# Output projection by seven block products, its weight parts made in the first block, norm scaling on VectorE

## The chip, the cores and the metric

The kernel runs on one core of one Trainium2 chip. The metric is the device time of one execution in microseconds (us).

## What is computed

One hybrid encoder layer over 1024 tokens of 1024 channels, in float32. The reference, cut to what matters here:

```
h = LN1(alpha*x + 0.5*SwiGLU_a(x))
h = LN2(alpha*h + HybridMixer(h))
h = LN3(alpha*h + 0.5*SwiGLU_b(h))

def swiglu(x, w_gate, w_up, w_down):
    return (silu(x @ w_gate) * (x @ w_up)) @ w_down

# end of HybridMixer (after attention and the Fourier branch):
    merged = g_attn * (attn @ w_proj_attn) + g_four * (four @ w_proj_fourier)
    return merged @ w_out
```

`merged @ w_out`, the output projection, is the product that the change rewrites. The hidden width of each SwiGLU is 2752.

## The kernel before

**Precision.** TensorE takes float32 rounded (fp32r). Each operand is cut into a high part (a copy, on ACT, L346) and a low part (a subtraction, on VectorE, L350). A product is then three matmuls: high by high, low by high, high by low. A "split" below is that pair of operations on a page of 128x1024.

**Stages on TensorE (PE), in order.** The first SwiGLU block ("a"): 21 pair jobs for gate and up, then its down projection. Norm 1 and the transposes of its result (tpY). The values, queries, keys and gates (q, s, v pairs) with the attention. The projections of the two branches (pj, pf). The output projection (wo, L2078). Norm 2 and its transposes (tpZ, L407). The second block ("b"), norm 3 and the output.

**The down projection of block a** is done by seven products of blocks (Strassen-Winograd) and not by eight. Products come in the order 1, 6, 2, 5, 3, 7, 4, and each has eleven steps, j = 0 to 10. Each step has 12 matmuls (four token tiles m, three terms), and needs one page qa, loaded by SP in two transfers of 256 KB (L815 and L816, `load_step`) and then split. qa53 is step 3 of product 5. Results stay in PSUM bank sets: products 5 and 3 share set Z. Product 3 is added onto product 5's sum, so what VectorE has to take out of product 5 alone must be read in between. That is `a_p5` (L923, one per token tile), which adds bank Z onto the right half of `ya` of tile m+4:

```
        def a_p5(m):
            y = Y[m + 4][:, R]
            stt(y, y, ALPHA, B[tag, "Z", m], op0=OP.mult, op1=OP.add)
...
            jd(3, 0).after((p5, -2.5))
```

`ya` is the residual, the input row tile (512 KB), loaded by SP (L1089) in two groups: tiles 0 to 3, then tiles 4 to 7. The last line makes product 3's first step wait for `a_p5`. `a_c12` (L927) takes the finished Z, and norm 1 of tiles 0 to 3 follows it: a mean (L988), a Square with its sum and a square root on ACT (L993, L995), a reciprocal and a product on VectorE (L1004, L1005), the scaling on ACT (L1008), then transposes on PE and their evacuation on ACT (L417).

**What sets the order.** A planner writes out a static list of instructions for each engine from costs and due times; on the chip, each engine works through its list in order, and so does SP with the loads. SBUF is cut into 46 pages of 512 KB, and a load waits until its page is free. The wait can thus be for PE, VectorE or a store of POOL.

**Parts kept in DRAM.** `keep_parts` loads a weight page, splits it early, lets POOL store both parts (two transfers of 512 KB) and reloads both when they are needed (1 MB). Before the change it serves the eight pages of the branch weights w_proj_attn and w_proj_fourier, and its early work is due at step 8 of product 2 (`early = J["a", "d", 2, 8]`), with a lead of 60 us.

**The output projection** has 16 jobs (two halves of the channels, eight token tiles) of 24 matmuls. Its weights wo are loaded and split just ahead of it; each job's two banks are added to the residual on VectorE (L2085, L2087). The second block's first six weight pages ("ld") are loaded and split around its start by `lead_weights`.

Of the kernel before, what the change touches and what calls it, by code (L numbers as in the profile page):

```python
# [16 lines left out]
P = 128  # L17
# [278 lines left out]
def kernel(  # L296
# [3 lines left out]
    w_proj_attn, w_proj_fourier, w_out, ln2_g, ln2_b, ffn2_gu, ffn2_tail,  # L300
# [8 lines left out]
    b_in, w_pa, w_pf, w_out = b_in[0], w_proj_attn[0], w_proj_fourier[0], w_out[0]  # L309
# [30 lines left out]
    def split(name, get, put, deps=(), need=None, lead=14.0, w=1024, pages=2, gives=1):  # L340

        st = {}

        def hi():
            st["h"] = page(name + "h", F32R)
            nc.scalar.activation(st["h"][:, :w], get()[:, :w], AF.Copy)  # L346
# [6 lines left out]
        if isinstance(need, tuple):  # L353

            def piece(i):
                cs, last = slice(i * 512, (i + 1) * 512), None

                def hi_():
                    if i == 0:
                        st["h"] = page(name + "h", F32R)  # L360
                    nc.scalar.activation(st["h"][:, cs], get()[:, cs], AF.Copy)

                def lo_():
                    if i == 0:
                        st["l"] = page(name + "l", F32R)
                        put((st["h"], st["l"]))
                    nc.vector.tensor_sub(st["l"][:, cs], get()[:, cs], st["h"][:, cs].bitcast(F32))
# [16 lines left out]
    class Operand:  # L384
# [12 lines left out]
        def turn(self, m, node, tile_of, c0):  # L397
# [11 lines left out]
            for q in range(2):  # L409
                n = f"a{hf + 1}{q + 1}"  # L410
                for i in range(2):
                    def evac(n=n, i=i, q=q):
                        if (n, i) not in self.raw:
                            self.raw[n, i] = page(f"{self.name}{n}{i}")
                        for j in range(2 * i, 2 * i + 2):
                            k = c0 + 4 * q + j
                            nc.scalar.activation(self.raw[n, i][:, (j % 2) * 512 + col * P:(j % 2) * 512 + (col + 1) * P],  # L417
                                                 ps[q][:, j, :], AF.Identity, bias=ln_cols[:, k + 8:k + 9],
                                                 scale=ln_cols[:, k:k + 1])
                    self.got.setdefault((n, i), []).append(S(0.56, evac, [f], frees=i, pages=1 if col == 0 else 0))  # L420

        def derive(self, first, whole, lead):
# [3 lines left out]
            def parts(n, i, deps, need, src=None, gives=0):  # L426
                self.node[n, i] = split(f"{self.name}{n}{i}", lambda: raw[src or n, i],
                                        lambda p: self.part.__setitem__((n, i), p), deps, need,
                                        lead if need is first.get(n) else 14.0, gives=gives)
                return self.node[n, i]  # L430
            for n in ("a11", "a12", "a21", "a22"):
                for i in range(2 if first[n] else 0):
                    if isinstance(got[n, i], tuple):
                        self.node[n, i] = parts(n, i, got[n, i], (first[n], first[n]))
                    else:
                        parts(n, i, got[n, i], first[n])
# [185 lines left out]
    def ffn(tag, X, w_gu, w_tail, w_dn, load_rest, norm, rest_deps=None, sums_at=None, by_tile=False):  # L622
# [5 lines left out]
        LEAD = 6  # L628
# [123 lines left out]
        for i, c in enumerate(ck[:LEAD]):  # L752
            lead_weights(c, w_gu, J[c0, 1], ((41.0 if i == 0 else 38.6 - 0.2 * i), 37.0 - 0.2 * i) if tag == "a" else None)
# [227 lines left out]
    def norm_head(acc, sums, deps, name, which):  # L981
# [14 lines left out]
        n = V(0.12, mean, deps)  # L996
        return st, n, S(1.7, dev, [n], pages=1)

    def norm_tile(acc, sums, deps, name, which):

        st, _, n = norm_head(acc, sums, deps, name, which)
# [5 lines left out]
        def scaled():  # L1007
            nc.scalar.activation(st["y"], st["a"], AF.Identity, bias=sums()[:, 2:3], scale=st["rs"])  # L1008
        n = V(0.3, shift, [n])
        return S(1.4, scaled, [n], gives=1), lambda: st["y"]  # L1010
# [50 lines left out]
    X1, X2, X3 = Operand("X"), Operand("Y"), Operand("Z")  # L1061
# [604 lines left out]
    branch_jobs((0, 1, 2, 3, 4), (0,))  # L1666
    branch_jobs((5,), (1, 2))
    branch_jobs((6,), (3,))
    branch_jobs((7,), (4, 5))
    for gi in range(2):  # L1670
        for m in range(8):
            WJ[gi, m] = job(24 * MM, None, 2, gives=16 if m == 7 else 0)
            if gi == 0 and m < 2:
                branch_jobs((), (6 + m,))
# [6 lines left out]
    def keep_parts(name, load, deps, fold_=None):  # L1681
# [22 lines left out]
        def again(key, need, lead):  # L1704
            def run():
                PW[key] = t = page(name + "h", F32R), page(name + "l", F32R)
                for i in range(2):
                    nc.sync.dma_start(t[i].bitcast(F32), dst[i])
            q = Q(need, 1.0, run, [(n, 6.0)], lead, pages=2)
            need.after(q)  # L1710
        return again
    PW, kept = {}, {}
    for c2 in range(4):
# [17 lines left out]
        kept["f", c2] = keep_parts(f"wpf{c2}", load_pf, [(rev_n, 20.0)], fold_w)  # L1731

# [245 lines left out]
    pj_n = {}  # L1978
# [23 lines left out]
    for c in range(8):  # L2002
# [27 lines left out]
        def sine(c=c, st=st):  # L2030
            st["q"] = half(f"pfq{c}")
            nc.scalar.activation(st["q"], st["s"], AF.Copy)

# [12 lines left out]
        def merge(c=c, st=st):  # L2046
            nc.vector.tensor_add(gates[0, c], gates[0, c], st.pop("f"))
        q = gate_load(1, c, FJ[c])
        n = S(0.62, sine, [FJ[c]], frees=1, halves=1)
        n = V(1.8, outs, [n], frees=2, hgives=1, pages=1)  # L2050
        n = V(1.23, gate, [n, q], gives=1)
        n = V(1.23, merge, [n] + pj_n[c], gives=1)
        split(f"mg{c}", lambda c=c: gates[0, c], lambda p, c=c: merged.__setitem__(c, p), [n],
              WJ[c // 4, 0], 100.0)


    wo = {}
    for k in range(8):
        def load(k=k):
            wo[k] = t = page(f"wo{k}")  # L2060
            nc.sync.dma_start(t, w_out[k * P:(k + 1) * P, :])
        split(f"wo{k}", lambda k=k: wo[k], lambda p, k=k: wo.__setitem__(k, p),
              [Q(WJ[k // 4, 0], 0.5, load, (), pages=1)], WJ[k // 4, 0])
    for m in range(8):
        st, sums = {}, kb.small([P, 4], "lw", bufs=9)

        def load(m=m, st=st):
            st["a"] = t = page(f"ya{m}")
            nc.sync.dma_start(t, y_spill[m])
        q = Q(WJ[0, m], 0.5, load, [(spilled[1, m], 5.0)], pages=1)  # L2070
        for gi in range(2):
            def run(gi=gi, m=m, st=st):
                st["b", gi] = bk = [bank(f"wo{gi}{m}{i}") for i in range(2)]
                ms = slice(m * P, (m + 1) * P)
                for k in range(4 * gi, 4 * gi + 4):
                    for ti, (a, b) in enumerate(TERMS):
                        for i in range(2):
                            nc.tensor.matmul(bk[i], pick(merged[k], a)[:, ms], pick(wo[k], b)[:, i * 512:(i + 1) * 512],  # L2078
                                             start=(k == 4 * gi and ti == 0), stop=(k == 4 * gi + 3 and ti == 2))
            WJ[gi, m].fn = run  # L2080

        def add(gi, i, m=m, st=st, sums=sums):
            a = st["a"][:, i * 512:(i + 1) * 512]
            if gi == 0:
                stt(a, a, ALPHA, st["b", 0][i], op0=OP.mult, op1=OP.add)  # L2085
            else:
                stt(a, st["b", 1][i], 1.0, a, op0=OP.mult, op1=OP.add, accum_out=sums[:, i:i + 1])  # L2087
        deps = []
        for i in range(2):
            n = V(0.69, lambda i=i, add=add: add(0, i), [WJ[0, m], q], frees=1)  # L2090
            deps.append(V(0.69, lambda i=i, add=add: add(1, i), [WJ[1, m], n], frees=1))
        n, y = norm_tile(lambda st=st: st["a"], lambda sums=sums: sums, deps, f"y2_{m}", 2)
        unit[2, m] = G(lambda m=m, y=y: pool_dma(n2_spill[m], y()), [n])
        X3.turn(m, n, y, 16)
# [7 lines left out]
    def rows2(ck):  # L2102
# [6 lines left out]
        rows2, lambda k: (J[PC["q", k], 1], J[PC["q", k], 4]), True)  # L2109
# [46 lines left out]
def _layouts(inputs):  # L2156
# [6 lines left out]
    for i in (1, 2):  # L2163
# [17 lines left out]
    out["c_ln"] = np.concatenate([a[f"ln{i}_{w}"].reshape(KD, P).T for i in (1, 2) for w in "gb"], 1)  # L2181
    out["in_values"] = v.transpose(3, 0, 2, 1, 4).reshape(3, 4, P, 1024)
# [4 lines left out]
        "w_proj_attn", "w_proj_fourier", "w_out", "ln2_g", "ln2_b", "ffn2_gu", "ffn2_tail",  # L2187
# [21 lines left out]
```

## Time and profile before

| what | value |
|---|---|
| time, median of 3 runs | 2071.83 us (2071.36 to 2073.81) |
| the profiled execution | 2072.24 us, span 2070.3 us |
| TensorE busy | 2058.5 us of the span, granted clock 0.999 |
| VectorE, ACT, POOL busy | 1276.4, 910.4, 233.6 us |
| down projection of block a, product 5 | 509.85 to 539.77 us |
| output projection, first to last matmul | 1339.7 to 1439.6 us |
| traffic | 401.29 MB, mean 194 GB/s |

A row of the stretches in the prediction gives a stretch, its length, each engine's busy time with the number of its instructions, the granted TensorE clock, the share of time that the 16 DMA engines are busy (a little over 1 where packets overlap) and GB/s. A row of the waits gives the instruction that waits, what it waits for, the sum, how often, and the longest. A timeline row begins with the start and the duration.

### The profile page before, as it was taken

Reading aid. Unit: us, or ns where it says so; the run is one execution under the profiler, and the core shown is the slowest. Engines: PE = TensorE matmul, PEld = TensorE weight load, DVE = VectorE, ACT = ScalarE, POOL = GpSimd, SP = SyncE. Lnnn points to the kernel's source line nnn. Section 1 sums busy time; section 2 is a strip of 40 time slices with the busy share of each in tenths; the row PEclk is TensorE's granted clock in tenths of the full one; section 3 lists DMA queues with packets and bytes.
Section 4 is the critical chain, followed back from the end, with each engine's and each line's share of the span. In section 5 each row is a group of like instructions: output and inputs, shape, how many; then the busy total and the mean of one; then the engine's idle time right before and its main releaser. Section 6 shows DMA issues by size and latency. Waiting matters only on the chain.

```text
span 2070.3 us, 25541 instructions
## 1 busy us (share of the span) xinstructions
PE 2058.5 (99%) x9523; PEld 1713.6 (83%) x9523; DVE 1276.4 (62%) x1757; ACT 910.4 (44%) x1441; POOL 233.6 (11%) x404
## 2 busy tenths in 40 slices
PE   9999999999999999999999999999999999999998
PEld 7888888888888888888888888888888888888887
DVE  7865555576554658455556764763877665575565
ACT  6433333555475324455455443318633333355342
POOL 0122111010000010021121111000011101010000
PEclk9999999999999999999999999999999999999999
DMA  5778875599743336467786659523144433357743
GB/s 203 236 239 260 253 220 169 177 341 404 257 160 120 102 122 182 142 178 204 207 218 198 226 185 384 184 97 138 60 169 179 157 132 127 123 202 273 263 159 105
DMA packets 151292, 401.29 MB, mean 194 GB/s; under 512 B 18338, under 2 KB 40690, under 8 KB 150720
## 3 DMA queue, kind: packets, MB, share of 16 engines
q1 hardware_dynamic: 111648, 266.38, 37.2%
q0 software_dynamic: 39520, 133.28, 21.5%
q8 instruction: 74, 1.21, 0.2%
q14 instruction: 50, 0.41, 0.1%
HBM read 303.41 MB, written 153.84 MB: 221 GB/s over the span
## 4 chain that ended last, share of the span: by engine, by line
PE 97%; ACT 1%; DMA 1%; DVE 0%; issue 0%; DVEq 0%; SPq 0%
PE Ab L462 14%; PE Aa L462 13%; PE Aq L462 8%; PE Da L462 6%; PE Db L462 5%; PE As L462 5%; PE wo L2078 3%; PE Dq L462 3%; PE Zb L827 3%; PE Xb L827 3%; PE Za L827 3%; PE Xa L827 3%; PE pj L1991 2%; PE v L1238 2%; PE Ds L462 2%; PE pv L1600 2%
## 5 line engine op out<-in xcount | busy, mean ns | idle before, releaser
L1568 ACT ACTIVATE p<-p,stat 128x192 f32<-128x192 f32 (+2 forms) x96 | 42.3, 442 | 17.0 <-DVE stat L1563 16.0
L326 POOL DMA_DIRECT2D hsaa<-t2a x21 | 12.0, 571 | 317.1 <-DVE t2a L696 299.0
L1358 DVE SCALAR_TENSOR_TENSOR oq<-Dq,b_cols,t2q 128x512 f32<-128x512 f32 x12 | 11.8, 986 | 50.8 <-PE Dq L462 50.8
L326 POOL DMA_DIRECT2D hsba<-t2b x21 | 11.4, 543 | 279.6 <-DVE t2b L696 279.6
L1600 PEld LDWEIGHTS pv<-pT,v 128*128 128x128 f32 (+1 forms) x320 | 37.3, 189 | 6.1 <-ACT pT L1589 1.0
L692 DVE TENSOR_TENSOR t2b<-Db,t2b 128x512 f32<-128x512 f32 x21 | 14.5, 691 | 44.9 <-PE Db L462 44.9
L692 DVE TENSOR_TENSOR t2a<-Da,t2a 128x512 f32<-128x512 f32 x21 | 14.5, 691 | 44.4 <-PE Da L462 44.4
L600 ACT ACTIVATE t2a<-Aa 128x512 f32<-128x512 f32 x21 | 12.6, 600 | 65.5 <-PE Aa L462 65.4
L1600 PE MATMUL pv<-pT,v 128*128 128x128 f32 (+1 forms) x320 | 40.8, 289 | 0.5 <-ACT pT L1589 0.5
L600 ACT ACTIVATE t2b<-Ab 128x512 f32<-128x512 f32 x21 | 12.6, 599 | 62.9 <-PE Ab L462 62.9
L1553 DVE SCALAR_TENSOR_TENSOR p<-sc,bias 128x512 f32<-128x512 f32 (+1 forms) x40 | 24.7, 620 | 25.0 <-PE sc L1539 20.6
L326 POOL DMA_DIRECT2D n_spill<-y x16 | 8.6, 538 | 264.5 <-ACT y L1008 264.5
L1539 PE MATMUL sc<-oq,oq 128*128 128x192 f32 (+2 forms) x192 | 34.1, 322 | 0.0
L684 DVE TENSOR_TENSOR t3a<-Da,t3a 128x512 f32<-128x512 f32 x21 | 14.5, 690 | 27.8 <-PE Da L462 26.4
L1539 PEld LDWEIGHTS sc<-oq,oq 128*128 128x128 f32 x192 | 29.8, 190 | 2.0
L1358 DVE SCALAR_TENSOR_TENSOR oq<-Dq,b_cols,t3q 128x512 f32<-128x512 f32 x12 | 11.8, 987 | 30.1 <-PE Dq L462 30.1
L462 PE MATMUL Db<-Zs40h,usb 128*128 128x512 f32 x84 | 29.4, 391 | 0.7 <-DVE t3b L684 0.7
L462 PE MATMUL Db<-Zs41h,usb 128*128 128x512 f32 x84 | 29.3, 389 | 0.0
L462 PE MATMUL Da<-Xs40h,usa 128*128 128x512 f32 x84 | 29.3, 389 | 0.0
L462 PE MATMUL Da<-Xs41h,usa 128*128 128x512 f32 x84 | 29.3, 389 | 0.0
L684 DVE TENSOR_TENSOR t3b<-Db,t3b 128x512 f32<-128x512 f32 x21 | 14.5, 690 | 20.7 <-PE Db L462 16.0
L1563 DVE TENSOR_REDUCE stat<-p 128x2 f32<-128x384 f32 (+2 forms) x40 | 24.5, 620 | 1.2
(7340 smaller groups left out, 7210.4 us busy)
## 6 DMA issues: line engine op xcount, KB each, us to landing
qa<-hsas SPq DMA_DIRECT2D x44, 256.0 KB, 5.9
qa<-tdat SPq DMA_DIRECT2D x44, 256.0 KB, 5.4
qb<-hsbs SPq DMA_DIRECT2D x44, 256.0 KB, 4.4
ga<-in_ffn_gu_dram SPq DMA_DIRECT2D x21, 512.0 KB, 6.1
ua<-in_ffn_gu_dram SPq DMA_DIRECT2D x21, 512.0 KB, 8.4
gb<-in_ffn_gu_dram SPq DMA_DIRECT2D x21, 512.0 KB, 3.5
ub<-in_ffn_gu_dram SPq DMA_DIRECT2D x21, 512.0 KB, 4.4
qa<-hsaa SPq DMA_DIRECT2D x33, 256.0 KB, 4.8
```

The lines of the kernel that those rows point to most:

```text
L326: nc.gpsimd.dma_start(*a, **kw)
L462: nc.tensor.matmul(out, pick(w, a)[:, k * P:(k + 1) * P], self.cols(xn, b, k), start=first and k == 0 and ti == 0, stop=last and k == 3 an ...
L600: nc.scalar.activation(H[c, t], B[c, "B"], AF.Copy)
L684: nc.vector.tensor_sub(H[c, "t3"], B[c, "D"], H[c, "t3"])
L692: nc.vector.tensor_sub(H[c, "t2"], B.pop((c, "D")), H[c, "t2"])
L827: nc.tensor.matmul(B[tag, set_, m], pick(q, a)[:, m * P:(m + 1) * P], pick(q, b)[:, R], start=first and j == 0 and ti == 0, stop=j == PAIR ...
L1238: nc.tensor.matmul(ps, X2.cols(f"a{hf + 1}{k // 4 + 1}", a, k % 4)[:, mm * P:(mm + 1) * P], pick(wv, b), start=(k == 0 and ti == 0), stop= ...
L1539: nc.tensor.matmul(sv[:, i, :], qk[0][:, qt * P:(qt + 1) * P], qk[1][:, k0:k0 + w], start=True, stop=True, skip_group_check=True)
L1568: nc.scalar.activation(p3()[:, i, :], p3()[:, i, :], AF.Exp, bias=stats[h][:, k, 0:1], scale=1.0, accum_out=stats[h][:, k, 1:2])
L1600: nc.tensor.matmul(out_of(tiles.index(qt)), env["v"][kc, rows], pt[r0:r0 + rows, sl * P:(sl + 1) * P], start=qt not in seen, stop=last, sk ...
L1991: nc.tensor.matmul(bk[hf], pick(wv, a)[:, k, cc * P:(cc + 1) * P], pick(attn[k], b)[:, hf * 512:(hf + 1) * 512], start=(k == 0 and ti == 0 ...
L2078: nc.tensor.matmul(bk[i], pick(merged[k], a)[:, ms], pick(wo[k], b)[:, i * 512:(i + 1) * 512], start=(k == 4 * gi and ti == 0), stop=(k == ...
```

## The change

1. **Seven products.** The output projection uses the same seven block products, in the order 1, 2, 6, 7, 5, 4, 3, each with four jobs of 12 matmuls. The merged operand becomes raw pages ("M"), with splits and 1024-wide combinations of blocks on VectorE (`X4.derive`). The sums of w_out's blocks are made on the chip, by a copy and an adding DMA each, during block a's pair jobs 13 to 17. Four copies on ACT seed the second bank of products 6 and 7 with product 1's result, and 24 additions on VectorE take the place of 32.

```
    WORDER = ((1, "A", True), (2, "A", False), (6, "B", False), (7, "B", False), (5, "D", True), (4, "B", False),
              (3, "D", False))
    for p, bk, new in WORDER:
        for m in range(4):
            WJ[p, m] = job(12 * MM, None, int(new), gives=8 if m == 3 else 0)
```

2. **Parts made in block a.** Fourteen parts of w_out (wob: blocks, wot: sums of blocks) and the second block's six pages (wl) go through `keep_parts`. The loads of wo and ld, and their splits, are gone from the place of use; reloads of 1 MB each stand there.

```
    lead2 = [keep_parts(f"wl{c}", lambda t, c=c: nc.sync.dma_start(t, ffn2_gu[c, 0]), [],
                        early=J["a", "d", 7, 8]) for c in range(LEAD)]
    for r, (p, _, _) in enumerate(WORDER):
        n = PROD[p][1]
        for i in range(2):
            kept["o", n, i] = keep_parts(f"wo{n}{i}", lambda t, n=n, i=i: nc.sync.dma_start(t, out_block(n)[i]),
                                         [wtn[n]] if n in wtn else [], early=J["a", "d", (5, 3, 7)[r // 3], 8])
```

3. **Norm 1 and norm 2.** The scaling moves from ACT to VectorE, and so does half of the evacuation of the transposes; the planner gets a slack for them, and norm 2 serves tiles 0 to 3 first.

```
-            nc.scalar.activation(st["y"], st["a"], AF.Identity, bias=sums()[:, 2:3], scale=st["rs"])
+            nc.vector.tensor_scalar(st["y"], st["a"], st["rs"], sums()[:, 2:3], op0=OP.mult, op1=OP.add)
...
+                            if q == 0:
+                                nc.scalar.activation(dst, ps[q][:, j, :], AF.Identity, bias=b_, scale=g_)
+                            else:
+                                nc.vector.tensor_scalar(dst, ps[q][:, j, :], g_, b_, op0=OP.mult, op1=OP.add)
```

Three places show how the order moves. In the lists, `[waits DMAHW..]` is a load's landing, `DMASW` a store's.

SP's loads just ahead of the second group of ya, before (qa_4191 is step 2 of product 3, qa_4208 and qa_4229 are steps 3 and 4):

```order
L815 DMA qa_4191<-hsas_174 128x512 [waits DMAHW1_49,DVE_49]
L816 DMA qa_4191<-in_ffn_down_dram 128x512 [waits DMAHW2_49]
L815 DMA qa_4208<-hsas_175 128x512 [waits DMAHW3_49,PE_49]
L816 DMA qa_4208<-in_ffn_down_dram 128x512 [waits DMAHW4_49]
L815 DMA qa_4229<-hsas_176 128x512 [waits DMAHW5_49,PE_49]
L816 DMA qa_4229<-in_ffn_down_dram 128x512 [waits DMAHW6_49]
L1089 DMA ya_4252<-in_x_dram 128x1024 [waits DMAHW7_49,PE_49]
```

and of the change (qa_4318 and qa_4335 are steps 3 and 4):

```order
L1768 DMA wot_4290<-wtt_259 128x1024 [waits DMAHW5_49,DVE_49]
L1768 DMA wot_4292<-wtt_259 128x1024 [waits DMAHW6_49,PE_49]
L1768 DMA wot_4294<-wtt_257 128x1024 [waits DMAHW7_49,DMASW2_49]
L1768 DMA wot_4296<-wtt_257 128x1024 [waits DMAHW0_49,DMASW4_49]
L1768 DMA wot_4298<-wtt_260 128x1024 [waits DMAHW1_49,DVE_49]
L1768 DMA wot_4300<-wtt_260 128x1024 [waits DMAHW2_49,DMASW5_49,DMASW0_49]
L827 DMA qa_4318<-hsas_175 128x512 [waits DMAHW3_49,DMASW7_49,DMASW6_49]
L828 DMA qa_4318<-in_ffn_down_dram 128x512 [waits DMAHW4_49]
L827 DMA qa_4335<-hsas_176 128x512 [waits DMAHW5_49,DMASW7_49]
L828 DMA qa_4335<-in_ffn_down_dram 128x512 [waits DMAHW6_49]
L1101 DMA ya_4356<-in_x_dram 128x1024 [waits DMAHW7_49,PE_49]
```

Six loads of parts have come between steps 2 and 3, some with waits for POOL's stores; a first group of six (wob and wot) stands further ahead, after step 2 of product 5.

VectorE at a_p5, before (L923):

```order
L350 TENSOR_TENSOR qa310l<-qa_4359,qa310h 128x1024 [waits DMAHW5_49,DMAHW6_49,DVE_49,Activation_49]
L350 TENSOR_TENSOR qa70l<-qa_4380,qa70h 128x1024 [waits DMAHW0_49,DMAHW7_49,DVE_49,Activation_49]
L923 SCALAR_TENSOR_TENSOR ya_4252<-ya_4252,Za_4263 128x512 [waits PE_49]
L923 SCALAR_TENSOR_TENSOR ya_4254<-ya_4254,Za_4264 128x512 [waits PE_49]
L923 SCALAR_TENSOR_TENSOR ya_4256<-ya_4256,Za_4265 128x512 [waits PE_49]
L923 SCALAR_TENSOR_TENSOR ya_4258<-ya_4258,Za_4266 128x512 [waits PE_49]
L350 TENSOR_TENSOR qa71l<-qa_4401,qa71h 128x1024 [waits DMAHW1_49,DMAHW2_49,DVE_49,Activation_49]
```

and of the change (L935):

```order
L350 TENSOR_TENSOR wot41el<-wot_4300,wot41eh 128x1024 [waits DMAHW2_49,Activation_49]
L350 TENSOR_TENSOR qa33l<-qa_4318,qa33h 128x1024 [waits DMAHW3_49,DMASW6_49,DMAHW4_49,DVE_49,Activation_49]
L350 TENSOR_TENSOR qa34l<-qa_4335,qa34h 128x1024 [waits DMAHW5_49,DMAHW6_49,DVE_49,Activation_49]
L935 SCALAR_TENSOR_TENSOR ya_4356<-ya_4356,Za_4367 128x512 [waits DMAHW7_49,PE_49]
L935 SCALAR_TENSOR_TENSOR ya_4358<-ya_4358,Za_4368 128x512 [waits DMAHW0_49,PE_49]
```

Before, the splits stood eleven and more steps ahead (product 7's first step) when a_p5 came, and a_p5 waited for PE alone; now the last split ahead of it is step 4 of product 3, and a_p5 waits for the landing of ya too.

VectorE at a_c12, of the change (L939; before, the split ahead of it was that of qa40):

```order
L350 TENSOR_TENSOR qa72l<-qa_4546,qa72h 128x1024 [waits DMAHW3_49,DMASW5_49,DMAHW4_49,DVE_49,Activation_49]
L350 TENSOR_TENSOR wl0el<-wl_4549,wl0eh 128x1024 [waits DMAHW5_49,PE_49,Activation_49]
L350 TENSOR_TENSOR wl1el<-wl_4551,wl1eh 128x1024 [waits DMAHW6_49,DVE_49,Activation_49]
L350 TENSOR_TENSOR wl2el<-wl_4569,wl2eh 128x1024 [waits DMASW7_49,DMAHW7_49,PE_49,Activation_49]
L350 TENSOR_TENSOR wl3el<-wl_4571,wl3eh 128x1024 [waits DMAHW0_49,DVE_49,Activation_49]
L350 TENSOR_TENSOR wl4el<-wl_4573,wl4eh 128x1024 [waits DMASW1_49,DMAHW1_49,PE_49,Activation_49]
L350 TENSOR_TENSOR wl5el<-wl_4575,wl5eh 128x1024 [waits DMAHW2_49,DVE_49,Activation_49]
L939 SCALAR_TENSOR_TENSOR ya_4214,lsa<-Za_4367,ya_4214 128x512 [waits PE_49]
```

The six splits of wl have come ahead of a_c12. On PE, the transposes of tiles 0 and 1 (tpY) now stand before step 3 of product 7; before, they stood after it.

More of the change, by code (lines that the diff above doesn't have):

```diff
@@ L308 @@
     x, out = x[0], out[0]
-    b_in, w_pa, w_pf, w_out = b_in[0], w_proj_attn[0], w_proj_fourier[0], w_out[0]
+    b_in, w_pa, w_pf, w_out = b_in[0], w_proj_attn[0], w_proj_fourier[0], out_blocks
     def as_k(t, kd=KD):
@@ L338, in pick, with split @@
         return parts[0 if kind == "hi" else 1]
-    def split(name, get, put, deps=(), need=None, lead=14.0, w=1024, pages=2, gives=1):
+    def split(name, get, put, deps=(), need=None, lead=14.0, w=1024, pages=2, gives=1, tokens=False):
         st = {}
@@ L353, in split, with cut @@
         if isinstance(need, tuple):
+            def cut(t, i):
+                return t.rearrange("p (k n) -> p k n", k=2)[:, :, i * 256:(i + 1) * 256] if tokens else t[:, i * 512:(i + 1) * 512]
             def piece(i):
[L356 removed]
                 def hi_():
@@ L979, in root_table, with norm_head @@
         S(1.5, lambda: nc.scalar.activation(t, eps, AF.Sqrt), [after_])
-    def norm_head(acc, sums, deps, name, which):
+    def norm_head(acc, sums, deps, name, which, slack=4.0):
         st = {}
@@ L995, in dev, with norm_tile @@
             nc.scalar.activation(st["rs"], s[:, 3:4], AF.Sqrt, bias=eps, scale=1.0 / D)
[L996 to L1001, printed above, removed]
+        n = V(0.12, mean, deps, slack=slack)
+        return st, n, S(1.75, dev, [n], pages=1, slack=slack)
+    def norm_tile(acc, sums, deps, name, which, slack=4.0):
+        st, _, n = norm_head(acc, sums, deps, name, which, slack)
         def shift():
@@ L1702, in keep_parts, with again @@
         fl.later(n, 6.0, gives=2)
-        def again(key, need, lead):
+        def again(key, need, lead, got=None):
             def run():
@@ L1712, with out_block, copy, add @@
     PW, kept = {}, {}
+    oblk = {f"b{kh + 1}{nh + 1}": w_out[2 * kh + nh] for kh in range(2) for nh in range(2)}
+    wt = {n: kb.dram([2, P, 1024], f"wt{n}") for n in ("t1", "t2", "t3", "t4")}
+    wtn = {}
+    def out_block(n):
+        return (oblk if n in oblk else wt)[n]
+    for i, (to, x0, x1) in enumerate((("t1", "b11", "b12"), ("t3", "b12", "b22"), ("t2", "t1", "b22"),
+                                      ("t4", "t2", "b21"))):
+        def copy(to=to, x0=x0):
+            nc.sync.dma_start(wt[to], out_block(x0))
+        def add(to=to, x1=x1):
+            pool_dma(wt[to], oblk[x1], accum_op=OP.add, max_dma_last_dim=4096)
+        n = Q(J[("a", 13 + i), 1], 1.0, copy, [wtn[x0]] if x0 in wtn else [], lead=0.0)
+        wtn[to] = Q(J[("a", 14 + i), 5], 1.0, add, [n], lead=0.0)
     for c2 in range(4):
@@ L2057 @@
[L2057 to L2063, printed above, removed]
-    for m in range(8):
[L2065 to L2092, printed above, removed]
@@ new lines, with run @@
+        n = V(1.38, merge, [n] + pj_n[c], gives=2, pages=2 if cc == 0 else 0)
+        for r in (1, 2):
+            X4.got.setdefault((f"a{r}{c // 4 + 1}", c % 4 // 2), []).append(n)
+    X4.derive({"a11": WJ[1, 0], "a12": WJ[2, 0], "a21": None, "a22": WJ[4, 0]}, {p: WJ[p, 0] for p in PROD}, 30.0)
+    for p, bk, new in WORDER:
+        xn, wn = PROD[p]
+        for i in range(2):
+            kept["o", wn, i](("o", wn, i), WJ[p, 0], 22.0 - 2.0 * i)
+        WJ[p, 0].after(X4.nodes(xn))
+        for m in range(4):
+            def run(p=p, bk=bk, new=new, m=m, xn=xn, wn=wn):
+                if new:
+                    B["w", bk, m] = bank(f"w{bk}{m}")
+                for k in range(4):
+                    w = [t[:, (k % 2) * 512:(k % 2) * 512 + 512] for t in PW["o", wn, k // 2]]
+                    for ti, (a, b) in enumerate(TERMS):
+                        nc.tensor.matmul(B["w", bk, m], X4.cols(xn, a, k)[:, m * P:(m + 1) * P], pick(w, b),
+                                         start=new and k == 0 and ti == 0, stop=k == 3 and ti == 2,
+                                         skip_group_check=True)
+            WJ[p, m].fn = run
```

130 lines of the change are left out of this document (96 added, 34 removed).

## The prediction

> **What bounds the kernel now.** I read the page first: busy shares, the traffic by slices, then the chain that ended last.
>
> ```profile
> span 2070.3 us, 25541 instructions
> PE 2058.5 (99%) x9523; PEld 1713.6 (83%) x9523; DVE 1276.4 (62%) x1757; ACT 910.4 (44%) x1441; POOL 233.6 (11%) x404
> GB/s 203 236 239 260 253 220 169 177 341 404 257 160 120 102 122 182 142 178 204 207 218 198 226 185 384 184 97 138 60 169 179 157 132 127 123 202 273 263 159 105
> PE 97%; ACT 1%; DMA 1%; DVE 0%; issue 0%; DVEq 0%; SPq 0%
> ```
>
> PE is busy for all but 11.8 us and is 97% of the chain. A matmul removed is time removed, unless something else then makes PE wait. The traffic row says where that could be: slices 9 and 10 (414 to 518 us) carry 341 and 404 GB/s, far over the mean. Next, PE's waits:
>
> ```profile
> PE Db L462 <- DVE t3b L684: 0.7, 1, 0.7
> PE tpZ L407 <- ACT y L1008: 0.6, 3, 0.2
> ```
>
> So the kernel holds no wait worth removing, and no slack that absorbs a new one. Last, the traffic around those two slices, which lie in the first block's down projection, where the change puts its new transfers (columns: stretch, length, busy time of each engine, PE clock, DMA share, GB/s):
>
> ```profile
> 430.00:460.00 30.00, 30.00 (x135) 24.82 (x134) 17.46 (x17) 14.76 (x14) 1.65 (x4) 1.00 1.08 328
> 460.00:490.00 30.00, 30.00 (x134) 24.86 (x133) 17.46 (x17) 13.26 (x15) 6.83 (x13) 1.00 1.04 413
> 490.00:520.00 30.00, 30.00 (x134) 24.85 (x133) 24.39 (x29) 17.20 (x17) 0.00 (x0) 1.00 1.04 396
> 520.00:540.00 20.00, 20.00 (x90) 16.53 (x89) 10.56 (x11) 11.46 (x11) 0.00 (x0) 1.00 0.98 342
> 540.00:580.00 40.00, 40.00 (x178) 33.14 (x177) 22.70 (x38) 18.70 (x24) 0.53 (x1) 1.00 0.58 183
> 580.00:640.00 60.00, 60.00 (x283) 50.17 (x282) 30.39 (x51) 34.85 (x63) 3.52 (x7) 1.00 0.34 123
> ```
>
> The DMA engines are full (share 0.98 to 1.08) until 540, and PE still never waits: SP is running ahead of it. That lead is the only cushion.
>
> **The matmuls removed.** One down product of 132 matmuls lasts from 509.85 to 539.77:
>
> ```profile
> 509.85 0.39 PE L827 MATMUL Za<-qa50h 128*128 128x512 f32 x1
> 539.77 0.39 PE L827 MATMUL Za<-qa30h 128*128 128x512 f32 x1
> ```
>
> 29.92/132 = 0.2267 us each; a step of 12 is 2.72. The output projection goes from 8×2×24 = 384 to 7×4×12 = 336 matmuls: 48×0.2267 = **−10.88 us**. The 0.6 us of tpZ's wait on ACT goes with the scaling that leaves ACT: **−0.6** (bounds −0.6 and +1, if VectorE is late instead).
>
> **Work added to VectorE in the projection.** Its rows:
>
> ```profile
> 1305.00:1340.00 35.00, 35.00 (x195) 30.58 (x195) 28.40 (x44) 12.48 (x16) 0.00 (x0) 1.00 0.44 160
> 1340.00:1440.00 100.00, 99.36 (x474) 82.62 (x473) 53.07 (x107) 47.78 (x91) 3.26 (x6) 1.00 0.31 114
> L2047 DVE TENSOR_TENSOR gl<-gl,prf 128x1024 f32<-128x1024 f32 x8 | 9.8, 1225 | 0.3
> L2087 DVE SCALAR_TENSOR_TENSOR ya<-wo,ya 128x512 f32<-128x512 f32 x16 | 10.5, 689 | 14.1 <-PE wo L2078 14.1
> L1880 DVE SCALAR_TENSOR_TENSOR fcl<-fp,f_se,fch x4: 352/352/353, 1290.3 to 1299.8; 128x128 fp32r<-128x128 f32 x4
> L1942 DVE CAST fmidT<-fmidT x1: 420/420/420, 1304.9 to 1304.9; 4x514 fp32r<-4x514 f32 x1
> ```
>
> VectorE has 81.5 us there now. Added: 8 wide combinations at 1.225 (9.8), 32 transposed evacuations of 128x128 out of PSUM at 0.352 (11.3), 8 scalings. No row shows a 1024-wide scaling from SBUF with one tensor input: twice the 514-wide cast gives 0.84, the two-input row 1.23, and I take 0.84, the nearer in kind (6.7). Gone: 8 of the 32 adds (5.5) and two of 16 splits (2.4). That makes 101 us in 124, 82%: a busy engine, not yet the bound. Walking PE's and VectorE's new orders side by side with these durations (an estimate), the tightest places are the second tile's normed rows, 0.7 us ahead of their transposes, and the copies into the third product's banks, 1.2 ahead. I cost this at 0, bounds 0 and +3 (0.4 us more on each of eight scalings).
>
> **The transfers added.** Twenty parts (14 of w_out, 6 of the second block) are each loaded (0.524 MB), split, stored (two of 0.524 MB) in the first block, and reloaded later (1.05 MB). The reloads add 21 MB in about 150 us around the projection, 140 GB/s on the 160 and 114 above: below 396, hidden. The sums of w_out's blocks add some 8.4 MB over 80 us in slices 4 and 5 (260 and 253 GB/s): about 360, hidden, bounds 0 and +2. The loads and stores in the full stretch are not hidden. Order there: 6 parts, seven steps, four ya, four steps, 6 parts, two steps, and only then the four ya that a_p5 (now L935) needs. a_p5 must read bank Z before product 3 writes to it. Before:
>
> ```profile
> L1089 SPq DMA_DIRECT2D ya<-in_x_dram x8: 328/328/333, 498.2 to 513.4; - x8
> DMA to landing us min/median/max: 5.9/6.9/7.8
> 537.93 2.73 DVE L923 SCALAR_TENSOR_TENSOR ya<-ya,Za 128x512 f32<-128x512 f32 x4 [3.80 <-PE Za L827]
> ```
>
> The last ya is issued at 513.4 and lands 6.9 later, at 520.3; the fourth a_p5 starts at 540.0 (537.93 plus three of 0.68). Margin: 19.7 us. Ahead of that landing the change puts 12 loads (6.29 MB) and the first group's 12 stores (6.29 MB). The engines carried 396 GB/s there without room left, so 12.58/0.396 = **31.8 us** later: 552.1, **12.1 us past the need**. The second group's stores can push in as well, up to 15.9 us more. That stores don't wait politely is in the trace, from 460 to 490, when the parts of w_pa and w_pf were stored:
>
> ```profile
> DMA packets 4709, 12.38 MB, mean 413 GB/s; under 512 B 529, under 2 KB 532, under 8 KB 4708
> q0 software_dynamic: 2096, 7.60, 62.2%
> q1 hardware_dynamic: 2612, 4.76, 41.2%
> 470.16 1.06 ACT L346 ACTIVATE qa25h<-qa 128x1024 fp32r<-128x1024 f32 x1 [2.57 <-DMA qa<-in_ffn_down_dram]
> 473.94 1.06 ACT L346 ACTIVATE qa26h<-qa 128x1024 fp32r<-128x1024 f32 x1 [0.77 <-DMA qa<-in_ffn_down_dram]
> ```
>
> POOL's stores (q0; columns: packets, MB, share) took 61% of the bytes; a step of SP's came every 3.8 us where PE uses one in 2.72. SP is also held back by pages: in the new order its loads of the second group wait for POOL's stores of the first. I take half of the second group's stores ahead, since their last splits come when the ya are already queued: **+20.0 us** (bounds 12.1 and 28.0).
>
> The Trainium skill, page "DMA: Bandwidth & Descriptors", section "Queues, rings and completion order", says that each DMA engine takes turns between queues with work, a packet at a time. The trace agrees: 2096 and 2612 packets, though the bytes stand 61 to 38. The same page, section "Specifications", limits a core's HBM traffic to about 358 GB/s; by that 12.58 MB would take 35.1 us and not 31.8, and the stall would be 3.3 longer. The row of 413 GB/s over 30 us speaks against it here, so the sum goes by 396.
>
> **The next thing late.** After a_p5 the new VectorE order puts six splits of the second block's weights (wl0 to wl5) ahead of a_c12, from which norm 1 and the transposes before product 7's fourth step follow:
>
> ```profile
> 567.85 0.69 DVE L927 SCALAR_TENSOR_TENSOR ya<-Za,ya 128x512 f32<-128x512 f32 x1 [7.56 <-PE Za L827]
> 573.64 0.16 DVE L1004 RECIPROCAL lnrs<-lnrs 128x1 f32<-128x1 f32 x1 [0.29 <-ACT lnrs L995]
> ```
>
> From 560 SP has 9 steps (4.7 MB) and six wl (3.1) to bring beside 3.1 to 6.2 of stores: 27.7 to 35.6 us, so the last wl is split at 590 to 598. a_c12 falls due at 567.9+20 = 587.9. Its rows are wanted 10.0 us after that (577.85: product 7 begins 29.92 after 539.77, and three steps follow) and take 7.4 (573.64, two small operations, a scaling): 2.5 us of cover. I take **+4 us**, bounds 0 and +8.
>
> **Sum**, against the profiled execution's own 2072.24 (the span and 1.94 around it, which stay; 0.41 over the median of 2071.83): 2072.24 −10.88 −0.6 +20.0 +4 = 2084.8, so **2085**. Bounds: 2072.24−11.5+12.1 = 2072.9 and 2072.24−11.5+28+8 = 2096.8.
>
> **The rivals.**
> *The stores give way* (faster). If SP's loads alone go first, the last ya lands at 520.3+15.9 = 536.2, inside the need of 540.0, and the whole −11.5 stands: 2060.8. It decides at 3.8×0.396 = 1.5 MB of stores ahead of that landing. For it: stores do queue, and took up to 15.2 us to land. Against it: the 61% above.
>
> ```profile
> wpa_d<-wpa1el POOLq DMA_DIRECT2D x1, 512.0 KB, 6.7
> wpf_d<-wpf3el POOLq DMA_DIRECT2D x1, 512.0 KB, 15.2
> ```
>
> Chance 0.15.
> *The stall about cancels the gain.* If half of the first group's stores go ahead (23.8 us), the last ya lands at 544.1, 4.1 late; with 4 to 8 at the norm: 2069 to 2073. Chance 0.15.
> *The third group hurts as well.* Its 16 stores (8.4 MB) at 7.60/30 = 253 GB/s last 33 us, in which product 7's steps come every 3.8 us and not 2.72: 8.8 steps × 1.06 = 9 us more, 2094. It decides once SP's lead is under three steps when product 7 begins. Chance 0.17.
> *Seven products don't shorten the projection* because VectorE becomes its bound: +3 on a case without the DMA stall, 2064. Against it: 82%. Chance 0.03.
> The forecast has 0.50.
>
> **How the numbers follow.** 2085 is the likeliest case. The range 2064 to 2098 leaves out the first rival (0.15) and about 0.05 above. A measurement here tells about 0.2% (4.1 us) from no change: faster means below 2067.7, the first and the last rival, 0.18; same is 2067.7 to 2076, the second, 0.15; slower 0.67.
>
> **What would show it.** Right: in the waits, a_p5 on VectorE waits some 20 us for the DMA of ya near 540, PE's Za waits on that a_p5, the DMA share stays at 1 to about 600 instead of 540, and a second, smaller PE wait stands at tpY or at product 7's steps; the projection is 10.9 us shorter and without waits. Wrong: ya landed before 540 with PE at 100% in the down projection (first rival), or PE waits at tpZ or at the third product's banks.

## The result, and the profile after

The changed kernel takes **2089.60 us** (median of 6 runs, 2087.29 to 2094.34) against 2071.86 us (6 runs, 2071.36 to 2073.81): a ratio of **1.0088, 95% interval 1.0075 to 1.0101**. It is slower, inside the range, 4.6 us over the forecast of 2085. The profiled execution took 2093.08 us, its span is 2091.0.

The page after, with the lines that answer to those of before:

```profile
span 2091.0 us, 25730 instructions
PE 2055.6 (98%) x9475; PEld 1707.6 (82%) x9475; DVE 1329.1 (64%) x1855; ACT 885.5 (42%) x1375; POOL 258.8 (12%) x448
GB/s 201 244 239 258 256 260 256 175 336 412 409 400 262 96 147 114 184 147 190 210 203 223 206 213 308 267 262 247 86 173 159 176 142 110 125 201 279 262 169 93
PE 87%; DMA 11%; DVE 1%; ACT 1%; issue 0%; SPq 0%; POOL 0%; DVEq 0%; ACTq 0%; POOLq 0%
```

PE's share of the chain has fallen from 97% to 87%, and DMA's has risen from 1% to 11%. Two slices far over the mean have become four (9 to 12, 418 to 627 us, 336 to 412 GB/s), and slices 6 and 7 rose from 220 and 169 to 260 and 256. PE's own waits:

```profile
PE Za L839 <- DVE ya L935: 19.6, 4, 17.0
PE Aa L470 <- ACT t3a L608: 3.6, 1, 3.6
PE Ua L839 <- DVE qa40l L350: 0.8, 1, 0.8
PE Ua L839 <- DVE qa41l L350: 0.7, 1, 0.7
PE tpY L409 <- DVE y L1020: 0.6, 2, 0.4
```

The first is a_p5, the bank that product 3 has to wait for. The second is new and was not forecast. No wait at tpZ is left. The stretches of the down projection:

```profile
490.00:520.00 30.00, 30.00 (x134) 24.86 (x133) 19.70 (x19) 14.87 (x14) 6.35 (x12) 1.00 1.04 410
520.00:540.00 20.00, 20.00 (x90) 16.57 (x89) 8.63 (x14) 5.99 (x6) 0.00 (x0) 1.00 1.04 409
540.00:580.00 40.00, 20.43 (x71) 14.86 (x71) 22.38 (x24) 15.62 (x16) 6.38 (x12) 0.70 1.03 403
580.00:640.00 60.00, 58.35 (x270) 47.41 (x269) 42.14 (x65) 37.80 (x54) 12.54 (x23) 1.00 1.03 402
```

The DMA share stands at 1.03 until 640 (before, 0.58 and 0.34 in the last two rows), and PE works 20.4 of the 40 us from 540 to 580, at a mean clock of 0.70. What a_p5 waited for, on its line and on the line that loads ya:

```profile
L935 DVE SCALAR_TENSOR_TENSOR ya<-ya,Za x4: 686/689/689, 561.6 to 569.2; 128x512 f32<-128x512 f32 x4
  DMA ya<-in_x_dram: 5.6, 4
...
L1101 SPq DMA_DIRECT2D ya<-in_x_dram x8: 327/328/333, 519.7 to 551.5; - x8
...
DMA to landing us min/median/max: 11.0/14.0/17.6
```

The last ya is issued at 551.5 (before: 513.4) and takes up to 17.6 us (before: 7.8). The fourth a_p5 starts at 569.2 instead of 540.0. VectorE's own wait for ya is only 5.6 us, because it stands at the splits of qa33 and qa34 first. Their loads come just ahead of ya in SP's queue and land late too:

```profile
560.24 1.23 DVE L350 TENSOR_TENSOR qa34l<-qa,qa34h 128x1024 fp32r<-128x1024 f32 x1 [2.56 <-ACT qa34h L346]
561.63 0.69 DVE L935 SCALAR_TENSOR_TENSOR ya<-ya,Za 128x512 f32<-128x512 f32 x1 [0.17 <-DMA ya<-in_x_dram]
```

Where the time went, by the first matmul of each stage in both traces:

| first matmul | before | after | later by |
|---|---|---|---|
| down projection of block a (qa10) | 420.1 | 425.6 | 5.5 |
| product 5 (qa50) | 509.9 | 515.3 | 5.4 |
| product 3 (qa30) | 539.8 | 562.5 | 22.7 |
| product 7 (qa70) | 569.7 | 599.5 | 29.8 |
| values | 633.1 | 665.7 | 32.6 |
| queries | 791.7 | 825.4 | 33.7 |
| branch projections (pj) | 1262.3 | 1296.0 | 33.7 |
| second block | 1439.6 | 1459.3 | 19.7 |
| its down projection | 1853.3 | 1873.8 | 20.5 |
| end of the span | 2070.3 | 2091.0 | 20.7 |

So: 5.5 in the pair jobs, 24.4 around a_p5, 3.9 from product 7 to the queries, −14.0 from the projections to the second block, and 0.8 lost again in the second block before its down projection.

### The profile page after: what moved, and what is told of

It reads as the page before. It is cut to its first block, busy times and chain, and to the rows that moved or that the text cites. A ratio compares the mean times of both kernels' runs of the same rounds, so it can differ in the third digit from the quotient of the medians.

```text
span 2091.0 us, 25730 instructions
## 1 busy us (share of the span) xinstructions
PE 2055.6 (98%) x9475; PEld 1707.6 (82%) x9475; DVE 1329.1 (64%) x1855; ACT 885.5 (42%) x1375; POOL 258.8 (12%) x448
## 4 chain that ended last, share of the span: by engine, by line
PE 87%; DMA 11%; DVE 1%; ACT 1%; issue 0%; SPq 0%; POOL 0%; DVEq 0%; ACTq 0%; POOLq 0%
PE Ab L470 14%; PE Aa L470 13%; PE Aq L470 8%; PE Db L470 5%; PE Da L470 5%; PE As L470 5%; DMA qa<-tdat 4%; PE Dq L470 3%; DMA qa<-in_ffn_down_dram 3%; PE Zb L839 3%; PE Xb L839 3%; PE pj L2029 2%; PE Ds L470 2%; PE v L1250 2%; PE wA L2118 2%; PE pv L1612 2%
## 5 line engine op out<-in xcount | busy, mean ns | idle before, releaser
L326 POOL DMA_DIRECT2D hsaa<-t2a x21 | 12.1, 574 | 313.4 <-DVE t2a L705 313.4
L1551 PEld LDWEIGHTS sc<-oq,oq 128*128 128x128 f32 x192 | 29.8, 190 | 2.0
```

Source lines behind the costliest of these rows:

```text
L326: nc.gpsimd.dma_start(*a, **kw)
L1551: nc.tensor.matmul(sv[:, i, :], qk[0][:, qt * P:(qt + 1) * P], qk[1][:, k0:k0 + w], start=True, stop=True, skip_group_check=True)
```

## Experiments

The theory: loads and stores added where the DMA engines are full make ya late. The rivals: the place of ya in SP's queue alone, the work of splitting wherever it is put, or the sums of w_out's blocks. Edits are against the changed kernel.

**The parts made elsewhere: e1.** 

```
-  early=J["a", "d", 7, 8])                       # wl
+  early=J[PC["q", 4 + c], 1])
-  early=J["a", "d", (5, 3, 7)[r // 3], 8])       # wob, wot
+  early=J[PC["q", 3 + r], 1])
```

> The twenty parts (load, splits, stores) leave the first block's down projection for the query pairs, where the DMA engines have room; reloads and projection stay. If the stall at a_p5 comes from these transfers in the full stretch, a_p5 waits for PE alone, PE's wait on it (19.6 us, 24 with the slow matmuls behind it) and the waits in products 7 and 4 (3) are gone, the 13 us of the output projection remain, and the 5.5 us late in the pair jobs remain: 2062 to 2066. Rival, that the reloads or the work in the attention stage cost as much: 2072 or more.

It took 2106.99 us (4 runs, ratio 1.0174, 1.0157 to 1.0191). The first half of the expectation held: no wait at a_p5, at product 7 or at product 4 is left. But the attention stage, where the parts went, lost more than was saved: from the first matmul of the queries to the first of the branch projections it takes 509.6 us, against 470.6 before the change. PE's waits:

```profile
PE pt L1596 <- ACT p L1580: 15.1, 6, 6.2
PE pv L1612 <- ACT pT L1601: 7.1, 3, 4.4
PE Aq L470 <- DVE gq9l L350: 3.9, 1, 3.9
```

and ACT's, from 870 to 1000:

```profile
ACT gq8h L346 <- DMA gq<-in_in_pairs_dram: 6.2, 1, 6.2
ACT wot10eh L346 <- DMA wot<-wtt: 4.9, 1, 4.9
```

pt and pv wait for the softmax on ACT; ACT stands at a split whose load has not landed, with the exponentials behind it in its order. The rival was right about the time: here the early work stood ahead of work that PE was waiting for.

**The order alone: e2.** The second group of ya goes ahead of the parts.

```
-                pages=1) for m in range(8)]
+                pages=1, lead=62.0 if tag == "a" and m >= 4 else 24.0) for m in range(8)]
```

> Only the second group of ya is moved: its loads stand ahead of both groups of parts in SP's order. If only the place of ya in the queue mattered, 24 us go: about 2065. My theory is that the bytes matter too: step 3 of product 3 then comes at about 560 where PE wants it at 554, and steps come every 3.8 us while the second group's stores run, so 12 us or so of the 24 come back as waits for steps: 2074 to 2081. Rival, that the bytes alone decide: 2087 or more.

2090.40 us (4 runs, ratio 1.0088, 1.0071 to 1.0105): no gain. The landing of ya no longer holds a_p5, yet PE waits for it:

```profile
PE Za L839 <- DVE ya L935: 10.8, 1, 10.8
PE tpY L409 <- DVE y L1020: 6.7, 3, 6.1
```

VectorE's order shows why:

```profile
553.17 1.23 DVE L350 TENSOR_TENSOR wot40el<-wot,wot40eh 128x1024 fp32r<-128x1024 f32 x1
555.07 1.23 DVE L350 TENSOR_TENSOR wot41el<-wot,wot41eh 128x1024 fp32r<-128x1024 f32 x1 [0.67 <-ACT wot41eh L346]
556.21 2.48 DVE L935 SCALAR_TENSOR_TENSOR ya<-ya,Za 128x512 f32<-128x512 f32 x4
...
569.21 1.23 DVE L350 TENSOR_TENSOR qa35l<-qa,qa35h 128x1024 fp32r<-128x1024 f32 x1 [5.27 <-DMA wot_d<-wot11el]
```

a_p5 now stands behind the six splits of the second group (the last two are shown). VectorE works through nine splits from 543.6 on, nearly without a pause, and comes to a_p5 at 556.2. A step's split later waits for a store to free its page. My 12 us of gain were wrong, and the time is on the side of the rival. But it was VectorE's order that held a_p5 here, so e2 shows only that the place of ya in SP's queue is not enough; it does not show that the bytes alone decide.

**The bytes: e4.** Only the high half of each new part is stored, and both reloads read that half, so the kernel leaves out the low half of these weights.

```
-            for i in range(2):
+            for i in range(ends):                # 1 for wl, wob and wot
                 pool_dma(dst[i], st["p"][i].bitcast(F32))
```

> Of each of the twenty parts only the high half is stored, and both reloads read it, so the low half of these weights is replaced: half of the stores (10.5 of 21 MB) are left out, loads and splits stay. If stores go ahead of SP's loads, the last ya lands 3.1 MB + 3.1 MB earlier at 396 GB/s, 16 us, and the wait at a_p5 shrinks from 19.6 to 2 to 6 us: 2069 to 2075. Rival, that stores give way to loads: no change, 2087 to 2093.

2075.54 us (8 runs, ratio 1.0019, 1.0009 to 1.0030): 14.1 us less than the change, half a microsecond over the range expected. The wait at a_p5 is down to

```profile
PE Za L839 <- DVE ya L935: 7.2, 2, 7.1
```

from 19.6. Loads, splits and order stayed and only stores went, so stores do hold up SP's loads. The rival that they give way is out. Pages that stores had not yet freed were not what held SP up: in the changed kernel, of SP's waits between 480 and 600, only 0.7 us are put down to a store, and nearly all others to its own earlier loads, which had not landed.

**The new wait in the pair jobs: e3.** PE's 3.6 us on t3a came at 350.4, behind this:

```profile
348.81 1.06 ACT L346 ACTIVATE ga18h<-ga 128x1024 fp32r<-128x1024 f32 x1 [6.83 <-DMA ga<-in_ffn_gu_dram]
349.77 0.58 ACT L608 ACTIVATE t3a<-Aa 128x512 f32<-128x512 f32 x1
```

Pair 18's weights were late. SP issued them late, after a copy of one of the sums that has to wait for POOL's adding DMA. Its waits between 300 and 352, and what it issued behind the longer one:

```profile
SPq L1738 <- DMA wtt<-in_out_blocks_dram: 50.0, 2, 32.8
338.23 0.47 SPq L1738 DMA_DIRECT2D wtt<-wtt  x1
338.81 0.52 SPq L544 DMA_DIRECT2D ga<-in_ffn_gu_dram  x1
339.42 0.39 SPq L544 DMA_DIRECT2D ua<-in_ffn_gu_dram  x1
```

In e3 the two later copies stand one and two pairs later:

```
+        i += max(0, i - 1)
         n = Q(J[("a", 13 + i), 1], 1.0, copy, [wtn[x0]] if x0 in wtn else [], lead=0.0)
```

> Only the DMA sums are spread: each later copy of a sum stands one or two pairs later, so that SP does not wait in its order for POOL's adding DMA. If that wait holds up pair 18's weights, the PE wait of 3.6 us on t3a goes. The time: the stall at a_p5 is set by the DMA engines, which are full since 430, so most of the 5.5 us should be given back there: 2086 to 2090. Rival, that the two add up: 2084. Rival, that the traffic of the sums and not the order delays the weights: the PE wait on t3a stays.

The wait on t3a is gone, and the down projection starts at 420.4 instead of 425.6. So the order, not the traffic of the sums, had held the weights up. The time was 2087.80 us (4 runs, 2086.92 to 2089.17). The wait at a_p5 stayed,

```profile
PE Za L839 <- DVE ya L935: 20.0, 4, 17.4
```

at 17.4 instead of 17.0 for its first part. I had expected the 5 us to be given back there, and they were not: the fourth a_p5 starts at 564.4 instead of 569.2, so the landing of ya moves with PE. The time lies in the range that I gave, but not for the reason that I gave. The spans of the two profiles differ by 3.6; the medians by 1.8, which the spread of the two kernels (7 and 2 us) does not resolve.

**A stage with room: e6, e7.** e3's sums, and w_out's parts made during the values' products (before: DMA share 0.34, ACT 56 us of 150); in e6 the second block's pages stay where they were before the change, in e7 they are made in the values too.

```
+  early=(VJ["g", 3], VJ[1, 2], VJ["g", 4], VJ["g", 7], VJ[6, 2], VJ[7, 2], VJ[5, 2])[r], lead=24.0)   # wob, wot
+    lead2 = None                                                                                         # wl, e6
+  early=(VJ["g", 5], VJ["g", 6], VJ[6, 0], VJ[7, 0], VJ[5, 0], VJ[4, 0])[c], lead=24.0)                  # wl, e7
```

> The fourteen parts of w_out are made during the values' products (about 630 to 790 us, DMA share 0.2 to 0.4 and ACT a quarter busy before the change), the six pages of the second block are loaded and split at their place of use as before the change, and the sums are spread as in e3. If the transfers cost only where the DMA engines are full, and the attention stage suffered in e1 from splits on ACT and VectorE ahead of its chain, nothing stalls now and the 13.2 us of the projection remain: 2057 to 2061. Rival, that the early work costs anywhere: 2065 or more.

> As e6, with the six pages of the second block made in the same stage too: six more loads, splits and stores (9.4 MB) there, six splits fewer at the second block's start. Expected the same as e6 within 2 us (2057 to 2062); if VectorE is short in the values' stage (20 splits are 24 us of the 50 that it has free), PE waits for a split of the values and the time is 2063 or more.

e6 took 2063.54 us (5 runs, ratio 0.9963, 0.9949 to 0.9977): faster than before, without a wait at a_p5, though 2.5 us over the range expected. e7 took 2070.38 (10 runs, ratio 0.9992, 0.9983 to 1.0002): the rival held, the six further pages made PE wait for splits of the values' own weights (6.9 us in four waits, the longest shown):

```profile
PE vB L1189 <- DVE wvt30l L350: 3.4, 1, 3.4
```

**The second block's pages: e10, e11.** As e6, with these six pages made in the gates' pairs (e10) or at the end of product 4 (e11).

```
+  early=J[PC["s", 1 + c], 1], lead=24.0)        # e10
+  early=J["a", "d", 4, 4 + c], lead=24.0)       # e11
```

> As e6, with the six pages of the second block made during the last pairs (the gates, 1144 to 1290 us before the change, where no softmax chain runs) and reloaded at the second block's start. e6 lost about 3 us after the second block's start against the change (from its first matmul to its down projection 417.6 us, the change 414.5), where it splits these pages on VectorE; if that is their cost, e10 gives 2058 to 2061. Rival, that the gates' stage has no room either: 2063 or more.

> As e10, with these six pages made at the end of the first block's down projection (product 4, 600 to 640 us), where the DMA engines have a share of 0.34 before the change and the loads of the steps are through. If only the full stretch up to 540 is closed to early work, 2058 to 2062, and no wait at a_p5; rival, that norm 1 and the steps of product 4 suffer there: PE waits at tpY or at product 4's steps, 2064 or more.

e10 took 2068.21 us (10 runs, ratio 0.9984, 0.9974 to 0.9994): the waits moved into the gates,

```profile
PE As L470 <- ACT As L603: 2.8, 2, 1.7
PE As L470 <- ACT gs16h L346: 2.4, 1, 2.4
```

so there the rival held. e11 took **2061.86 us (4 runs, ratio 0.9953, 0.9936 to 0.9969)**, as expected and below both kernels. Its stretches:

```profile
540.00:580.00 40.00, 40.00 (x179) 33.09 (x179) 26.80 (x43) 17.80 (x24) 1.06 (x2) 1.00 0.63 204
580.00:640.00 60.00, 60.00 (x282) 50.19 (x281) 44.15 (x77) 32.38 (x49) 9.76 (x18) 1.00 0.87 316
640.00:790.00 150.00, 149.33 (x674) 123.52 (x673) 112.33 (x153) 59.87 (x79) 30.48 (x56) 1.00 0.68 249
```

The share in the last two rows was 0.34 before and is 0.87 and 0.68 now. What making the twenty parts costs can be read between the first matmuls of product 5 and of the queries: 281.8 us before, 310.1 in the change, 283.1 in e11 (511.7 to 794.8). So the same parts cost 28.3 us in the change and 1.3 us here. The span of e11 is 9.8 below that of before: 14.1 gained from the projections to the second block, less the 1.3, 1.8 in the pair jobs and 1.2 elsewhere. No run has the seven products with w_out's parts loaded and split at their place of use, so what making them early is worth stays open.

**Part 3 alone: e9, e12.** e6 and e10 with the scaling and all evacuations on ACT.

```
-            nc.vector.tensor_scalar(st["y"], st["a"], st["rs"], sums()[:, 2:3], op0=OP.mult, op1=OP.add)
+            nc.scalar.activation(st["y"], st["a"], AF.Identity, bias=sums()[:, 2:3], scale=st["rs"])
...
-                            if q == 0:
+                            if True:
```

> As e6, with part 3 of the change undone: the scaling of norm 1 and norm 2 and all evacuations of transposes on ACT again. If VectorE is the tight engine of the projection and ACT has room, this costs nothing or gains a little (2057 to 2061); if the chain of a norm on ACT sets when the transposes can go, PE's waits at tpZ return, up to 0.6 us for each of four tiles and more behind it: 2061 to 2064.

> As e10, with part 3 of the change undone (scaling of norms 1 and 2 and all evacuations of transposes on ACT). In e9 that cost 21 us, nearly all of it at the second block's start, where ACT also split the second block's pages. If those splits were what made ACT late, e12 loses only a little to e10, 1 to 5 us; if the norm itself is what ACT has no time for, it loses 10 or more.

The expectation for e9 was far too low: it took 2084.62 us (4 runs), 21.1 more than e6. e12 took 2080.70 (4 runs, 2078.71 to 2083.00), 12.5 more than e10, so the second of its two cases held. The stretch at the second block's start, e12 and then e10 (busy: PE, weight load, VectorE, ACT, POOL):

```profile
1420.00:1500.00 80.00, 72.77 (x343) 58.08 (x341) 41.70 (x69) 70.82 (x134) 3.76 (x8) 1.00 0.31 110
```

```profile
1420.00:1500.00 80.00, 80.00 (x383) 66.92 (x382) 66.18 (x115) 54.20 (x96) 4.29 (x8) 1.00 0.39 142
```

With the scaling on ACT, ACT is busy 70.8 of 80 us and PE idles 7.2; on VectorE both have room. So in these kernels part 3 is what lets norm 2 be ready in time. That the seven products make this necessary, by bringing the norms of eight tiles closer to the second block's start, is argued and not shown: no run undoes part 3 without them. (The planner lays out the rest of the order anew in such an edit, so a part of the 12 us may be that.)

**The clock: e8.** In the changed kernel the matmuls behind the wait are slow, and the clock says so (rows of 1 us; the last column but two is the clock, still 1.00 up to 549):

```profile
549.00:550.00 1.00, 0.00 (x0) 0.00 (x0) 1.00 (x1) 0.97 (x1) 0.90 (x2) 0.68 1.04 418
550.00:551.00 1.00, 0.00 (x0) 0.00 (x0) 0.94 (x2) 0.09 (x1) 0.69 (x2) 0.50 1.06 422
```

```profile
545.04 0.39 PE L839 MATMUL Za<-qa510h,qa510l 128*128 128x512 f32 x1
562.47 0.77 PE L839 MATMUL Za<-qa30h 128*128 128x512 f32 x1 [17.04 <-DVE ya L935]
563.03 0.63 PE L839 MATMUL Za<-qa30l,qa30h 128*128 128x512 f32 x1
563.46 0.63 PE L839 MATMUL Za<-qa30h,qa30l 128*128 128x512 f32 x1
564.87 0.80 PE L839 MATMUL Za<-qa30h 128*128 128x512 f32 x1 [0.79 <-DVE ya L935]
...
569.92 0.80 PE L839 MATMUL Za<-qa30h 128*128 128x512 f32 x1 [0.87 <-DVE ya L935]
...
573.39 0.40 PE L839 MATMUL Za<-qa31h,qa31l 128*128 128x512 f32 x1
573.62 0.39 PE L839 MATMUL Za<-qa31h 128*128 128x512 f32 x1
```

Four microseconds after PE's last matmul (its idle time begins at 545.4) the clock falls from 1.00 to 0.50; matmuls come every 0.43 us instead of 0.23 until 573.4, 10.9 us after work resumes. e8 fills the wait:

```
+        def keep_warm():
+            t = bank("kept_warm")
+            for _ in range(150):
+                nc.tensor.transpose(t[:, :P], ident, ident)
...
+            if p == 3 and tag == "a":
+                job(0.0, keep_warm, 1, frees=1)
```

> The change as it is, with 150 transposes of the identity ahead of product 3 on PE, into a bank that is free: they fill about 16 of the 17 us that PE waits for a_p5, and compute nothing that is used. If PE's idle time is what lowers its clock, the first 18 matmuls of product 3 then come every 0.23 us and not every 0.43, and 4 to 5 us go: 2084 to 2086. Rival, that the clock falls for another reason, or that filler costs what it saves: 2087 to 2093.

2089.74 us (4 runs, 2086.23 to 2093.66): no gain, on the side of the rival. The mechanism showed, the worth that I gave it did not:

```profile
560.68 0.39 PE L839 MATMUL Za<-qa30l,qa30h 128*128 128x512 f32 x1
560.91 0.40 PE L839 MATMUL Za<-qa30h,qa30l 128*128 128x512 f32 x1
562.79 0.72 PE L839 MATMUL Za<-qa30h 128*128 128x512 f32 x1 [1.48 <-DVE ya L941]
563.31 0.63 PE L839 MATMUL Za<-qa30l,qa30h 128*128 128x512 f32 x1
```

Behind the filler the first matmuls come every 0.23 us, so idle time is what lowers the clock. But the four ya land 2.5 us apart, PE waits three times more, and the clock falls again at 563, 3.9 us after the end of the filler (559.1), although three matmuls ran in between.

The low clock was also worth less than the 4 to 5 us that I expected. In the change PE goes at the pace of the landings until the fourth a_p5 is through: faster matmuls would have waited longer for the next ya. Half the clock costs time only from 569.92 to 573.39, where eight matmuls take 3.47 us and not 1.81: 1.7 us.

## Why the prediction was right, and where it was not

- **What bounds the kernel, and the cushion.** Right: SP's lead was the only slack, and the DMA share stays at 1.03 to 640 (forecast: about 600).
- **a_p5, +20.0 (12.1 to 28.0).** Right in place and mechanism, too small: the term came out at 24.4. PE's waits there sum to 19.6, but that they lie so close to 20.0 is chance, since the matmuls between them also come late. Counted as the forecast counts, by the fourth a_p5: the matmul behind it starts at 569.92 instead of 541.81, 28.1 later, of which 5.4 came along from the pair jobs. That leaves 22.7; the low clock behind it adds 1.7. The Trainium skill, page "TensorE: Matmul & The Clock Gate", section "Part 1: The HAM clock gate (the "warmup" mystery)", says that an idle window of some 3.4 us halves the clock. The traces agree with the half (0.50), about 4 us into the long wait and behind a wait of 3.6 us in the pair jobs. I had not looked for it.
- **That half of the second group's stores go ahead.** Too few. The fourth a_p5 starts 29.2 late, less the 5.4 from the pair jobs 23.8; in the prediction's own sum (12.1, and up to 15.9 more) that is about three quarters of these stores. That the stores' traffic delays ya, e4 bears out (half of the stores gone, 12.4 us less of the wait). The pages that SP was to wait for as well played hardly a part (0.7 us).
- **The next thing late, +4 (0 to 8).** The size was right (3.9) by luck, for the place was wrong. a_c12 starts at 597.6, with PE's last matmuls of product 3, and not behind wl5. The waits are at tpY (0.6), at product 4's first steps (0.8 and 0.7) and small ones.
- **The sums, 0 (0 to 2).** Wrong: 5.5. I priced their bytes as hidden and overlooked their order: SP's copy waits for POOL's adding DMA, and pair 18's weights are queued behind it. 3.6 is the wait, nearly all of the rest the clock, which fell there too. e3 showed it. The place was off as well: the sums run from 248 to 345 us, in slices 5 to 7, and not in slices 4 and 5.
- **Matmuls −10.88, tpZ −0.6.** Right in kind, 1.7 too small: −13.2 in all, with the 0.8 that was lost again in the second block. 10.9 are matmuls, 0.6 the waits at tpZ, 0.7 a wait of Db that is gone too; about 1 us is not assigned.
- **VectorE in the projection, 0 (0 to 3).** Right: no wait at tpZ or at the seeded banks. That ACT was the engine which part 3 had to relieve, I had not seen: e9 and e12.
- **The rivals.** Stores giving way: out by e4. The stall cancelling the gain: out, a_p5 alone cost more. The third group: its stores did hold steps up, but by about 2 us (0.2, 0.8 and 0.7 of waits at qa710, qa40 and qa41) and not 9. Seven products not shortening the projection: out by the −14.0.

The sum of the measured terms: 5.5 + 24.4 + 3.9 − 14.0 + 0.8 = 20.6, against 20.84 between the two profiled executions. So the range held with room, but the forecast of 2085 was 8.1 below the profiled execution of 2093.08: a_p5 (4.4) and the sums (5.5) cost more than forecast, and the gain of the projection was 1.7 larger.

## What to carry to other kernels

Work that is "made early" is not free because it is early: price its loads and its stores against the DMA share of the stretch where it lands, and look for the one transfer behind them in the queue that an engine needs at a fixed time. The same parts cost 28.3 us where the share already stood near 1 and 1.3 us where it was 0.34. In the attention stage (0.70 before, from 790 to 1102) they cost 39.0 us, because the split of a late load stands ahead of the softmax in an engine's order. A stage shortened on PE brings the work of the others closer together: check which of them has to be relieved with it.

## What the runs showed of the hardware

- TensorE's granted clock fell to 0.50 about 4 us after PE's last matmul (545.4 to 549.4). Behind a wait of 3.6 us in the pair jobs the matmuls ran at half pace for about 3.4 us. It also fell in e8 (559.1 to 563), where three matmuls ran in the stretch without much work.
- It stayed at half while PE worked in bursts of three matmuls with waits of about 0.8 us between them, and came back 10.9 us after work resumed, 3.5 us after the last of these waits (569.92 to 573.39).
- With the loads and stores of the parts beside them, the loads of ya took 14.0 us from issue to landing (median) instead of 6.9; with half of the stores left out (e4), 11.1.
